# A weighted sum over eight experts: separate two-row tiles replaced by a ten-row ring

## The chip, the cores and the metric

The kernel runs on one core of a Trainium2 chip. The metric is the device time of one execution in microseconds (us). Before the change it is 721.33 us, the median of 9 runs (721.25 to 721.79).

## What is computed

Each of 16 x 1024 = 16384 tokens has eight expert outputs of 512 fp32 values and eight weights. The output is their weighted sum:

```
batch, seq, n_experts, expert_dim = 16, 1024, 8, 512
weights = combine_weights[..., np.newaxis]
return np.sum(expert_outputs * weights, axis=2).astype(np.float32)
```

So 268.4 MB of expert outputs and 0.5 MB of weights are read, and 33.6 MB are written. Every value read is used once, in one multiplication and one addition.

## The kernel before

The tokens are laid over 128 partitions. I call 128 tokens, one on each partition, a **token row**; there are 128 of them, and a row holds 16 KiB of expert outputs per partition. The loop goes over 64 steps of J = 2 rows. A step's input tile `in_t` holds both rows (32 KiB per partition, 4 MiB in all); since a partition's two tokens follow each other in memory, the tile is one contiguous piece of HBM.

*Loads.* `issue_load(m)` (L53 to L63) issues step m's load on SP where m is even and on ACT where it is odd (L56), and a small weight load (8 KB) on POOL (L60). The last two steps' tiles are loaded row by row (L59). Loads are issued three steps ahead (LA = 3) into four buffers, so a load waits until VectorE has finished the step four before it.

*Arithmetic.* For each of the two rows VectorE multiplies expert 0 by its weight (L77, tensor_scalar) and then adds the seven others one by one (L83, scalar_tensor_tensor: out = in * weight + acc). Each of these reads the `acc` that the one before has just written.

*Stores.* The step's result, 4 KiB per partition, is stored by the queue that did not load this step (L92).

*The last two steps* are split between engines: ACT makes the products of experts 4 to 7 in bf16 (L111), VectorE sums experts 0 to 3 (L116, L122), adds the bf16 products in pairs (L130, L135) and to `acc` (L138), and each row is stored by itself from SP (L141).

Each engine works through its own instructions in order. On SP and ACT a load or store that waits holds up what is issued behind it. The code sets no other order.

Of the kernel before, what the change touches and what calls it, by code (L numbers as in the profile page):

```python
# [1 line left out]

# [4 lines left out]


@with_exitstack  # L10
def kernel(
    ctx: ExitStack,
    tc: tile.TileContext,
    expert_outputs: bass.AP,
    combine_weights: bass.AP,
    out: bass.AP,
):
    nc = tc.nc
    fp32 = mybir.dt.float32
    bf16 = mybir.dt.bfloat16  # L20

    B, S, E, D = expert_outputs.shape
    T = B * S
    P = 128
    J = 2
    n_steps = T // (P * J)

    eo_blk = expert_outputs.rearrange("b s e d -> (b s) e d").rearrange(
        "(n p j) e d -> n p j e d", p=P, j=J
    )  # L30
    w_blk = combine_weights.rearrange("b s e -> (b s) e").rearrange(
        "(n p j) e -> n p j e", p=P, j=J
    )
    o_blk = out.rearrange("b s d -> (b s) d").rearrange(
        "(n p j) d -> n p j d", p=P, j=J
    )

    in_pool = ctx.enter_context(tc.tile_pool(name="in_pool", bufs=4))
    w_pool = ctx.enter_context(tc.tile_pool(name="w_pool", bufs=4))
    out_pool = ctx.enter_context(tc.tile_pool(name="out_pool", bufs=4))  # L40
    prod_pool = ctx.enter_context(tc.tile_pool(name="prod_pool", bufs=2))

    ES = E // 2
    K_TAIL = 2

    load_engines = [nc.sync, nc.scalar]

    LA = 3
    in_tiles: list[bass.AP | None] = [None] * n_steps
    w_tiles: list[bass.AP | None] = [None] * n_steps  # L50

    def issue_load(m: int) -> None:
        in_t = in_pool.tile([P, J, E, D], fp32, name="in_t")  # L53
        w_t = w_pool.tile([P, J, E], fp32, name="w_t")
        if m < n_steps - K_TAIL:
            load_engines[m % 2].dma_start(out=in_t, in_=eo_blk[m])  # L56
        else:
            for j in range(J):
                load_engines[m % 2].dma_start(out=in_t[:, j], in_=eo_blk[m, :, j])  # L59
        nc.gpsimd.dma_start(out=w_t, in_=w_blk[m])  # L60
        in_tiles[m] = in_t
        w_tiles[m] = w_t

    for m in range(min(LA, n_steps)):
        issue_load(m)

    for n in range(n_steps):
        if n + LA < n_steps:
            issue_load(n + LA)
        if n >= n_steps - K_TAIL:  # L70
            continue
        in_tile = in_tiles[n]
        w_tile = w_tiles[n]
        acc = out_pool.tile([P, J, D], fp32)

        for j in range(J):
            nc.vector.tensor_scalar_mul(  # L77
                out=acc[:, j, :],
                in0=in_tile[:, j, 0, :],
                scalar1=w_tile[:, j, 0:1],  # L80
            )
            for e in range(1, E):
                nc.vector.scalar_tensor_tensor(  # L83
                    out=acc[:, j, :],
                    in0=in_tile[:, j, e, :],
                    scalar=w_tile[:, j, e : e + 1],
                    in1=acc[:, j, :],
                    op0=mybir.AluOpType.mult,
                    op1=mybir.AluOpType.add,
                )  # L90

        load_engines[(n + 1) % 2].dma_start(out=o_blk[n], in_=acc)  # L92

    tail_steps = list(range(n_steps - K_TAIL, n_steps))
    tail_accs = {}
    tail_prods = {}
    for n in tail_steps:
        acc = out_pool.tile([P, J, D], fp32, name="acc")
        prods = prod_pool.tile([P, J, E - ES, D], bf16, name="prods")
        tail_accs[n] = acc  # L100
        tail_prods[n] = prods

    for j in range(J):
        for n in tail_steps:
            in_tile = in_tiles[n]
            w_tile = w_tiles[n]
            acc = tail_accs[n]
            prods = tail_prods[n]

            for e in range(ES, E):  # L110
                nc.scalar.mul(  # L111
                    out=prods[:, j, e - ES, :],
                    in_=in_tile[:, j, e, :],
                    mul=w_tile[:, j, e : e + 1],
                )
            nc.vector.tensor_scalar_mul(  # L116
                out=acc[:, j, :],
                in0=in_tile[:, j, 0, :],
                scalar1=w_tile[:, j, 0:1],
            )  # L120
            for e in range(1, ES):
                nc.vector.scalar_tensor_tensor(  # L122
                    out=acc[:, j, :],
                    in0=in_tile[:, j, e, :],
                    scalar=w_tile[:, j, e : e + 1],
                    in1=acc[:, j, :],
                    op0=mybir.AluOpType.mult,
                    op1=mybir.AluOpType.add,
                )
            nc.vector.tensor_add(  # L130
                out=prods[:, j, 0:2, :],
                in0=prods[:, j, 0:2, :],
                in1=prods[:, j, 2:4, :],
            )
            nc.vector.tensor_add(  # L135
                out=prods[:, j, 0, :], in0=prods[:, j, 0, :], in1=prods[:, j, 1, :]
            )
            nc.vector.tensor_add(  # L138
                out=acc[:, j, :], in0=acc[:, j, :], in1=prods[:, j, 0, :]
            )  # L140
            nc.sync.dma_start(out=o_blk[n, :, j], in_=acc[:, j, :])  # L141


# [1 line left out]
_INS = ['expert_outputs', 'combine_weights']  # L145
_OUTS = [((16, 1024, 512), 'float32')]


# [23 lines left out]
```

## Time and profile before

| What | Value |
|---|---|
| median of 9 runs | 721.33 us |
| the profiled execution | 721.3 us |
| its span, first to last instruction | 719.5 us |
| VectorE busy | 644.3 us, 1020 instructions |
| ACT busy | 11.4 us |
| L83, one scalar_tensor_tensor of 128x512 f32 | 744 ns, 868 of them |
| L77, one tensor_scalar of 128x512 f32 | 482 ns, 124 of them |
| L111, one ACT multiplication of 128x512 | 710 ns, 16 of them |
| DMA mean over the span | 421 GB/s, 302.63 MB |

The span lies inside the time of the execution; some 1.8 us are around it. "Busy" is the time in which an engine executes, and VectorE, ACT, POOL and SP are separate engines that run beside each other. SP does no arithmetic here, it issues DMAs. All DMAs, whoever issues them, are carried out by the same 16 DMA engines; the profile's DMA share is their mean busy share. A DMA is made of packets; the trace has a record of each packet with its start, length, size and queue, but not with its engine. Where the profile gives what ended an instruction's wait, it names the last event before it.

### The profile page before, as it was taken

The page shows a single profiled execution, that of the slowest core. Times are in us where ns is not written, and L with a number is a line of the kernel's source. Part 1 is how long each engine was busy: PE and PEld are TensorE (multiplying, and loading weights), DVE is VectorE, ACT ScalarE, POOL GpSimd, SP SyncE. Part 2 cuts the span into 40 slices and gives each one's busy share as a digit, 9 for nine tenths or more (in the row PEclk, how much of TensorE's full clock was granted, in tenths as well). Part 3 has the DMA queues.
Part 4 walks back from the last instruction along what each step waited for, and adds up shares of the span by engine and source line. Part 5 has one row for each costly group of instructions (what it writes and reads, how often), then busy time and mean ns, then how long its engine had stood idle before and what let it go on. Part 6 is the DMA issues. An engine that isn't in the chain of part 4 may idle for free.

```text
span 719.5 us, 1532 instructions
## 1 busy us (share of the span) xinstructions
DVE 644.3 (90%) x1020; ACT 11.4 (2%) x17; POOL 35.6 (5%) x68
## 2 busy tenths in 40 slices
DVE  0799999999998999989998999989998999999977
ACT  0000000000000000000000000000000000000023
POOL 1000000000000000000000000000000000000000
DMA  9999999999999999999999999999999999999993
GB/s 380 438 413 443 433 432 431 428 424 427 429 435 445 434 424 427 428 431 428 435 442 431 431 427 427 425 437 441 430 429 429 425 428 434 432 437 433 419 363 139
DMA packets 21068, 302.63 MB, mean 421 GB/s; under 512 B 3136, under 2 KB 4160, under 8 KB 12608
## 3 DMA queue, kind: packets, MB, share of 16 engines
q1 hardware_dynamic: 9792, 151.52, 49.3%
q10 hardware_dynamic: 9216, 150.47, 49.0%
q0 software_dynamic: 2048, 0.53, 0.3%
q14 instruction: 12, 0.10, 0.0%
HBM read 268.96 MB, written 33.55 MB: 420 GB/s over the span
## 4 chain that ended last, share of the span: by engine, by line
DMA 64%; DVE 35%; issue 1%; DVEq 0%; SPq 0%
DMA out_dram<-acc 56%; DVE acc L83 30%; DMA in_t<-in_expert_outputs_dram 8%; DVE acc L77 3%; DVE acc L122 1%; DVE acc L138 0%; DVE prods L130 0%; DVE acc L116 0%; DVE prods L135 0%; DVEq L77 0%; DVEq L116 0%; SPq L92 0%
## 5 line engine op out<-in xcount | busy, mean ns | idle before, releaser
L83 DVE SCALAR_TENSOR_TENSOR acc<-in_t,w_t,acc 128x512 f32<-128x512 f32 x868 | 580.1, 744 | 0.0
L77 DVE TENSOR_SCALAR acc<-in_t,w_t 128x512 f32<-128x512 f32 x124 | 54.6, 482 | 66.2 <-DMA in_t<-in_expert_outputs_dram 43.4
L60 POOL DMA_DIRECT2D w_t<-in_combine_weights_dram x64 | 35.4, 554 | 637.7 <-DVE acc L83 636.9
L111 ACT ACT_TABLE_LOAD x1 | 1.3, 1283 | 690.5 <-DMA in_t<-in_expert_outputs_dram 690.5
L111 ACT ACTIVATE prods<-in_t,w_t 128x512 bf16<-128x512 f32 x16 | 10.1, 710 | 9.3 <-DMA in_t<-in_expert_outputs_dram 9.3
L122 DVE SCALAR_TENSOR_TENSOR acc<-in_t,w_t,acc 128x512 f32<-128x512 f32 x12 | 8.8, 743 | 0.0
L116 DVE TENSOR_SCALAR acc<-in_t,w_t 128x512 f32<-128x512 f32 x4 | 1.9, 480 | 5.3 <-DMA out_dram<-acc 5.3
L138 DVE TENSOR_TENSOR acc<-acc,prods 128x512 f32<-128x512 f32 x4 | 2.7, 685 | 0.0
L130 DVE TENSOR_TENSOR prods<-prods 128x1024 bf16<-128x1024 bf16 x4 | 2.7, 683 | 0.0
L135 DVE TENSOR_TENSOR prods<-prods 128x512 bf16<-128x512 bf16 x4 | 1.7, 416 | 0.0
L156 POOL MEMSET const-float32-0.0<- 128x1 f32 x1 | 0.1, 99 | 0.2 <-issue 0.2
L156 POOL MEMSET const-bfloat16-1.0<- 128x1 bf16 x1 | 0.1, 102 | 0.0
L156 POOL MEMSET const-float32-1.0<- 128x1 f32 x1 | 0.1, 99 | 0.0
L156 POOL MEMSET const-uint8-127<- 128x1 uint8 x1 | 0.1, 99 | 0.0
## 6 DMA issues: line engine op xcount, KB each, us to landing
in_t<-in_expert_outputs_dram ACTq DMA_DIRECT2D x31, 4096.0 KB, 33.5
in_t<-in_expert_outputs_dram SPq DMA_DIRECT2D x31, 4096.0 KB, 33.3
out_dram<-acc ACTq DMA_DIRECT2D x31, 512.0 KB, 33.5
out_dram<-acc SPq DMA_DIRECT2D x31, 512.0 KB, 33.3
in_t<-in_expert_outputs_dram SPq DMA_DIRECT2D x2, 2048.0 KB, 31.2
in_t<-in_expert_outputs_dram ACTq DMA_DIRECT2D x2, 2048.0 KB, 14.0
w_t<-in_combine_weights_dram POOLq DMA_DIRECT2D x64, 8.0 KB, 6.8
out_dram<-acc SPq DMA_DIRECT2D x4, 256.0 KB, 2.7
```

The lines of the kernel that those rows point to most:

```text
L60: nc.gpsimd.dma_start(out=w_t, in_=w_blk[m])
L77: nc.vector.tensor_scalar_mul(out=acc[:, j, :], in0=in_tile[:, j, 0, :], scalar1=w_tile[:, j, 0:1],)
L83: nc.vector.scalar_tensor_tensor(out=acc[:, j, :], in0=in_tile[:, j, e, :], scalar=w_tile[:, j, e : e + 1], in1=acc[:, j, :], op0=mybir.Al ...
L111: nc.scalar.mul(out=prods[:, j, e - ES, :], in_=in_tile[:, j, e, :], mul=w_tile[:, j, e : e + 1],)
L116: nc.vector.tensor_scalar_mul(out=acc[:, j, :], in0=in_tile[:, j, 0, :], scalar1=w_tile[:, j, 0:1],)
L122: nc.vector.scalar_tensor_tensor(out=acc[:, j, :], in0=in_tile[:, j, e, :], scalar=w_tile[:, j, e : e + 1], in1=acc[:, j, :], op0=mybir.Al ...
L130: nc.vector.tensor_add(out=prods[:, j, 0:2, :], in0=prods[:, j, 0:2, :], in1=prods[:, j, 2:4, :],)
L135: nc.vector.tensor_add(out=prods[:, j, 0, :], in0=prods[:, j, 0, :], in1=prods[:, j, 1, :])
L138: nc.vector.tensor_add(out=acc[:, j, :], in0=acc[:, j, :], in1=prods[:, j, 0, :])
L156: nc = _bacc.Bacc("TRN2", target_bir_lowering=False, num_devices=1)
```

## The change

The tiles are replaced by one **ring** of ten token rows in SBUF (`SLOTS = 10`, 160 KiB per partition). Each partition now holds eight consecutive tokens (G = 8) of a group of 1024, so that neighbouring partitions of one load lie 128 KiB apart in HBM.

- *Weights.* All 128 rows' weights are loaded by one DMA at the beginning, on SP, in runs of 256 bytes.
- *Loads.* All on SP, in program order (`pin`): up to four rows (64 KiB per partition) in one DMA, less where the ring or a group of eight ends. Rows 112 to 125 come in pairs, row 126 in two pieces of four experts, row 127 in pieces of 3, 2, 2 and 1 experts. A load waits until VectorE has finished the rows that held its slots.
- *Short rows.* Rows 48 and 72 (`SHORT`) are each loaded as four DMAs of 120, 1, 2 and 5 partitions; their neighbours 49 and 73 are loaded by themselves, with one DMA each.
- *First term.* For rows 0 to 119 ACT multiplies expert 0 by its weight into `acc`, two rows ahead of VectorE.
- *Two chains.* VectorE takes the rows in pairs and alternates between them, term by term.
- *Last eight rows.* For rows 120 to 127 ACT scales an identity matrix by the weights of experts 0 to 2 (three diagonals), TensorE multiplies expert rows by these diagonals in fp32 and sums them in PSUM, and VectorE adds the other five terms, the first of them to the sum in PSUM.
- *Stores.* Eight rows at once (16 KiB per partition) on ACT, then rows 120 to 123 on ACT, 124 and 125 on SP, and 126 and 127 each by itself on SP.

The core of the diff (the old loops, printed above, go altogether; lines that only define names are cut):

```diff
+    G = 8
+    N = T // (P * G)
+    T_P = N * G
+    SLOTS = 10
+    PE_TOKENS = 8
+    SHORT = (48, 72)
+    PE_EXPERTS = 3
...
+    x = expert_outputs.rearrange("b s e d -> (b s) e d").rearrange(
+        "(n p g) e d -> n p g e d", p=P, g=G
     )
...
+    ring = one.tile([P, SLOTS, E, D], fp32, name="ring")
+    acc = one.tile([P, 2 * G, D], fp32, name="acc")
+    w_t = one.tile([P, T_P, E], fp32, name="w_t")
+    ident = one.tile([P, P], fp32, name="ident")
...
+    BULK = 112
+    t = 0
+    while t < BULK:
+        m = min(4, SLOTS - t % SLOTS, G - t % G)
+        if t in SHORT or t - 1 in SHORT:
+            m = 1
+        loads += [(t, m, 0, E)]
+        t += m
+    for t in range(BULK, T_P - 2, 2):
+        loads += [(t, 2, 0, E)]
+    loads += [(T_P - 2, 1, 0, 4), (T_P - 2, 1, 4, 8)]
+    loads += [(T_P - 1, 1, 0, 3), (T_P - 1, 1, 3, 5), (T_P - 1, 1, 5, 7), (T_P - 1, 1, 7, 8)]
...
+    def load_until(t):
+        nonlocal loaded
+        while loaded < len(loads) and loads[loaded][0] + loads[loaded][1] <= t:
+            i, m, e0, e1 = loads[loaded]
...
+            parts = (0, 120, 121, 123, P) if i in SHORT else (0, P)
+            for p0, p1 in zip(parts, parts[1:]):
+                pin(nc.sync.dma_start(out=dst[p0:p1], in_=src[p0:p1]))
+            loaded += 1
...
+    def first(i):
+        s, a = i % SLOTS, i % (2 * G)
+        if i < T_P - PE_TOKENS:
+            pin(nc.scalar.mul(out=acc[:, a], in_=ring[:, s, 0], mul=w_t[:, i, 0:1]))
+            return
+        ps = ps_pool.tile([P, D], fp32, name="ps")
+        for e in range(PE_EXPERTS):
+            diag = diag_pool.tile([P, P], fp32, name="diag")
+            pin(nc.scalar.mul(out=diag, in_=ident, mul=w_t[:, i, e : e + 1]))
+            nc.tensor.matmul(
+                ps, lhsT=diag, rhs=ring[:, s, e], start=e == 0, stop=e == PE_EXPERTS - 1
+            )
+        sums[i] = ps
...
+    def term(i, e):
...
+            before, e0 = (sums[i] if e == PE_EXPERTS else acc[:, a]), PE_EXPERTS
+        if e >= e0:
+            pin(
+                nc.vector.scalar_tensor_tensor(
+                    out=acc[:, a],
+                    in0=ring[:, s, e],
+                    scalar=w_t[:, i, e : e + 1],
+                    in1=before,
+                    op0=mult,
+                    op1=add,
+                )
+            )
...
+    pin(nc.sync.dma_start(out=w_t.rearrange("p (n g) e -> p n (g e)", g=G), in_=w))
+    make_identity(nc, ident)
+    load_until(SLOTS - 2)
+    for i in (0, 1):
+        first(i)
+    for i in range(0, T_P, 2):
+        load_until(i + SLOTS)
+        for k in (i + 2, i + 3):
+            if k < T_P:
+                first(k)
+        for e in range(E):
+            for k in (i, i + 1):
+                term(k, e)
+        end = i + 2
+        if end <= T_P - G and end % G == 0:
+            store(end - G, G, nc.scalar)
+        elif end == T_P - 4:
+            store(end - 4, 4, nc.scalar)
+        elif end == T_P - 2:
+            store(end - 2, 2, nc.sync)
+        elif end == T_P:
+            store(end - 2, 1, nc.sync)
+            store(end - 1, 1, nc.sync)
```

## The prediction, made before the change was run

> **What bounds the kernel now.** I read the page's totals first, then the table of stages, the chain of work that ended last, the timeline of the end, and the trace's records of single DMA packets.
>
> ```profile
> span 719.5 us, 1532 instructions
> ...
> DVE 644.3 (90%) x1020; ACT 11.4 (2%) x17; POOL 35.6 (5%) x68
> ...
> DMA  9999999999999999999999999999999999999993
> ...
> q14 instruction: 12, 0.10, 0.0%
> ```
>
> The line "q14" must be read with its header (packets, MB, share): the code itself is fetched by 12 DMA packets.
>
> ```profile
> core 0: us, DVE busy (x) ACT busy (x) POOL busy (x), PEclk, DMA share, GB/s
> ...
> 360.00:540.00 180.00, 165.14 (x261) 0.00 (x0) 8.55 (x16) 1.00 1.00 430
> ...
> 675.00:692.00 17.00, 16.28 (x27) 1.53 (x2) 0.00 (x0) 1.00 0.91 373
> 692.00:708.60 16.60, 11.27 (x21) 7.33 (x13) 0.00 (x0) 1.00 0.82 322
> 708.60:719.50 10.90, 7.29 (x13) 2.55 (x4) 0.00 (x0) 1.00 0.20 77
> ```
>
> Columns: stretch, its length, busy time of each engine, TensorE clock, DMA share, GB/s. VectorE is 90% busy, but DMA is 100% busy (430 GB/s) until 675 us and only then thins out. The chain gives the pace:
>
> ```profile
> 186.72 0.88 DVE acc L77 x2
> ...
> 629.01 0.88 DVE acc L77 x2
> ```
>
> These are 40 steps of two token rows apart: 442.3/40 = 11.06 us per step, where VectorE needs 2x0.40 + 14x0.663 = 10.08 (in the timeline a chained STT, the scalar_tensor_tensor of L83, starts 0.663 us after the one before, 744 ns long each). So VectorE waits for buffers, and DMA sets the pace.
>
> The packet records say why 11.06. A 2 KiB packet takes 85 ns, 4 KiB 159, 16 KiB 611, 32 KiB 1213: 37.6 ns per KiB plus some 9 ns, of which half overlaps with the neighbour. A 128-partition load leaves eight packets and one completion record on each of 16 engines. Summed, a step is 10.96 us, and fifteen engines keep that pace (their completions come every 10.96). One engine lags: its completion comes 0.8 us after the first at 64 us of the span, 1.8 at 142, 4.2 at 386, 6.5 at 673 (about 5.8 behind the fifteenth). Each step of the lag sits where a 309 ns code packet passes. That lag is the 0.1 us between 10.96 and 11.06.
>
> ```profile
> 690.60 0.82 ACTq L59 DMA_DIRECT2D in_t<-in_expert_outputs_dram  x2
> ...
> 708.59 2.56 ACT L111 ACTIVATE prods<-in_t,w_t 128x512 bf16<-128x512 f32 x4 [2.44 <-DMA in_t<-in_expert_outputs_dram]
> ...
> 715.23 0.69 DVE L138 TENSOR_TENSOR acc<-acc,prods 128x512 f32<-128x512 f32 x1
> ```
>
> The end: ACT issues the last two loads only at 690.6, when an earlier load of that queue has landed; DMA drains meanwhile (33 GB/s from 690.5 to 692.5). The last load lands at 708.6, VectorE ends at 715.9, the last store at 719.5. The profiled execution took 721.3, 1.8 more than its span, and the median is 721.33, so I add 1.8 and need no other correction.
>
> **The change, term by term.** I add up one ordinary DMA engine until the last load has landed, then the tail.
>
> *Start.* The first packet moved at 1.8 us. Now the weights go first on SP: 2048 runs of 256 bytes, 128 per engine. By the fit one costs 9 + 9.4 = 18 ns, together 2.4 us; from above, if the issue of sixteen times as many runs takes sixteen times the 0.33 us of a load, 5.3. I take 2.4, the fit's, since today's 512-byte packets (27 ns) lie on it. The 64 small weight loads on POOL (27 ns per engine each, 1.7 us) go.
>
> *Loads.* The bytes stay: 128 rows x 8 partitions x 16 KiB = 16384 KiB, x 37.6 ns = 616.5 us. One queue instead of two: from 685 to 688 us only SP's ring had loads and ran 16 KiB packets at 611 ns, so one queue loses nothing.
>
> *Stores.* 2048 KiB per engine, 77.1 us; 1920 KiB, 72.2 us, belong to rows up to 119 and lie before the last load, and 2.4 us (rows 120 to 123) too. In packets of 16 KiB instead of 4 KiB there are 152 instead of 512 per engine, which at half of 9 ns saves 1.6. All remaining packets, some 550, cost 2.5 us of such overhead.
>
> *Short rows.* A row as 120+1+2+5 partitions: 128 partitions are 16x8 in the trace; I take 120 as 15x8, so that one engine is spared 8 packets per row, and the eight rest on the first engines, at most 3 on one. Twice: 16x0.611 = 9.8 us spared, at most 6x0.611 = 3.7 us added. If the spared engine is the lagging one, its 5 to 6 us are more than gone, and 3.7 binds instead: 2.1 us better than not splitting. From above: if 120 partitions used fewer engines (eight with 15 packets), 2x7x0.611 = 8.6; if the wrong engine is spared, 3.7+5.8 = 9.5 on the laggard.
>
> Until the last load: 1.8 + 2.4 + 616.5 + 72.2 + 2.4 + 2.5 + 3.7 + 0.6 (last packet to release, as at the first load) = **702.1**. There is no drain as at 690: all loads sit on SP, which issues nothing else until the end, and wait only for ring slots.
>
> *Does the ring keep DMA fed?* A four-row load needs rows ten earlier finished. When four rows land, VectorE needs 0.7 + 28x0.663 = 19.3 us for them; six more rows in the ring are 29 us of loads. So 9.7 us of loads are left at the next issue, less 1.1 us from issue to packets and at most 6 of lag: some 3 us of cover. VectorE has 880 STT, 583 us; per pair of rows 9.3 against 10.9 of DMA. The two chains in turn bring nothing: an STT between foreign instructions in the tail (705.00 to 705.67) also takes 0.67. The multiplications move to ACT: 120x0.71 = 85 us on an idle engine. ACT's stores wait for VectorE with later multiplications behind them, which VectorE needs one pair (9.3 us) later. If the 3 us of cover were gone, each four-row load would add what is missing.
>
> *At nothing.* The identity (POOL) and the 24 scaled copies of it (ACT, at most 24x0.71 = 17 us) are made long before TensorE needs them, ACT's 1.3 us table load falls before the first landing, and the bf16 products and their sums (L111 to L138) go; without that cover a diagonal would delay its product by 0.7.
>
> *Tail.* The first piece of row 127 lands 1.25 MiB before the last, 3.0 us at 432 GB/s: 699.1. Then TensorE makes three products and VectorE, whose order puts row 127's first term second, has nine STT of 0.663 left, 6.1 us with the last one's end. Then 3.6 us, as today from VectorE's end to the span's. No row shows a matmul of 128x512 f32. [...] I take 0.74, the STT's that it replaces: 2.2. Sum: 699.1 + 2.2 + 6.1 + 3.6 = 711.0, + 1.8 = **712.8 us**, against 721.3.
>
> [...] The trace has no matmul and its clock column tells nothing of one. [...] For addresses, loads that were contiguous now step 128 KiB from partition to partition. [...]
>
> **Rivals.**
> 1. *TensorE paces the end (the slow side).* Behind rows 120 and 121 there are six rows (4.85 us each) and 3 MiB of stores (7.3), 36 us, so these rows land at 666. From there 24 products in sequence: 666 + 24m + 0.1 + 6.1 + 3.6 + 1.8. [...] For it: nothing in the trace prices fp32 products; against it: ACT and VectorE do 128x512 in 0.4 to 0.74.
> 2. *Strided loads, or stores beside them, are slower.* Break-even is 8.5/616.5 = 1.4%. For it: from 701.5 to 703.5 us 16 KiB load packets took 864 to 993 ns beside stores. Against it: 16 KiB pieces at 32 KiB pitch at 611. At 3% it gives 731.
> 3. *The split does not do what it says:* the lagging engine is not spared. 5.8 us more: 718.6.
> 4. *Weights at their upper price, products of 1.0 to 1.4 us:* 714 to 718.
> 5. *Less lag, a shorter tail than summed:* 708 to 710.
>
> **Chances.** Forecast (710 to 714.5) 0.45; rival 4 0.14; rival 3 0.10; rival 5 0.12; rival 1 0.08, of which 0.04 is slower and 0.02 the same; rival 2 0.11, of which 0.09 is slower and 0.01 the same; of rival 3 0.01 is the same. A measurement here tells about 0.2%, 1.4 us, from no change. Together: slower 0.13, same 0.04, faster 0.83. The range 708 to 721 leaves out rival 2, rival 1's slow half and the ends.
>
> **What would show it.** DMA share of 1.00 up to about 690 us; last load landing near 702; VectorE's end some 5 us later; a matmul group near 0.7 us; span near 711. A load landing on schedule with VectorE waiting for matmuls speaks for rival 1; load packets over 1213 ns per 32 KiB for rival 2; one engine's completions 5 us late for rival 3. Waits of VectorE with DMA idle in mid-span would refute the ring's cover.

## The result, and the profile after

The changed kernel takes 737.46 us (median of 10 runs, 735.85 to 745.96) against 721.38 us of the kernel before beside it. The ratio is 1.0235 with a 95% interval from 1.0219 to 1.0252: 2.4% slower, where I had forecast 1.2% faster. The profiled execution has a span of 735.1 us, 24.1 us more than the 711.0 that the terms gave.

The page of the changed kernel (busy times, then the 40 slices of 18.4 us each):

```profile
span 735.1 us, 1389 instructions
...
PE 27.7 (4%) x48; PEld 11.2 (2%) x48; DVE 585.7 (80%) x880; ACT 87.0 (12%) x145; POOL 0.7 (0%) x6
...
DMA  9999999999999999999999999999999999999992
GB/s 371 449 414 411 438 449 419 440 421 439 453 420 436 431 259 436 453 423 444 423 419 374 288 423 452 421 421 446 416 457 413 441 428 426 437 429 436 427 386 97
DMA packets 12023, 302.59 MB, mean 412 GB/s; under 512 B 3182, under 2 KB 3182, under 8 KB 4078
```

The row of DMA digits says that nothing is wrong: busy in every slice but the last. The row below says where the time is. The rate falls to 259 in one slice and to 374 and 288 in two others; elsewhere, the start and the end apart, it swings around 430 as before. The first dip is where row 48 is loaded, the second where row 72 is: the two **short rows**. The table of stages around the first dip (stretch, length, busy times, clock, DMA share, GB/s):

```profile
240.00:258.00 18.00, 0.00 (x0) 0.00 (x0) 17.69 (x27) 2.11 (x4) 0.00 (x0) 1.00 0.99 426
258.00:278.00 20.00, 0.00 (x0) 0.00 (x0) 13.96 (x22) 3.28 (x5) 0.00 (x0) 1.00 0.97 269
278.00:300.00 22.00, 0.00 (x0) 0.00 (x0) 14.90 (x23) 0.72 (x1) 0.00 (x0) 1.00 1.00 430
```

A share of 0.97 at 269 GB/s means that the engines are not idle, their packets take longer. The packet records agree: 611 ns is the usual length of a 16 KiB packet; of the 256 of rows 48 and 49 only 82 keep to it, 91 take 1130 to 1280 ns, and the longest takes 1775. Against the usual lengths the excess is 6.8 us per engine from 260 to 280 us and 9.2 from 390 to 420, together 16.0.

The other part that the change rebuilt is the end. The timeline:

```profile
712.10 12.23 PE L104 MATMUL ps<-ring,diag 128*128 128x512 f32 x24 [3.69 <-DMA ring<-in_expert_outputs_dram]
...
716.65 0.75 DVE L117 SCALAR_TENSOR_TENSOR acc<-ring,w_t,ps 128x512 f32<-128x512 f32 x1 [2.15 <-PE ps L104]
...
719.23 0.75 DVE L117 SCALAR_TENSOR_TENSOR acc<-ring,w_t,ps 128x512 f32<-128x512 f32 x1 [1.83 <-PE ps L104]
...
719.89 5.38 DVE L117 SCALAR_TENSOR_TENSOR acc<-ring,w_t,acc 128x512 f32<-128x512 f32 x8
...
725.19 1.40 DVE L117 SCALAR_TENSOR_TENSOR acc<-ring,w_t,ps 128x512 f32<-128x512 f32 x2
...
726.51 5.38 DVE L117 SCALAR_TENSOR_TENSOR acc<-ring,w_t,acc 128x512 f32<-128x512 f32 x8
```

Rows 124 and 125 are there at 711.94; VectorE waits for TensorE's first sum until 716.65 and then has twenty terms, with one more wait of 1.83 us, until 731.9. Each fp32 product is two matmul records, 0.855 us apart in the first part of the burst and 0.43 in the second, where the clock column goes from 0.57 to 1.00 (the third number from the right):

```profile
712.00:716.00 4.00, 3.90 (x5) 1.65 (x6) 2.50 (x4) 1.08 (x4) 0.00 (x0) 0.57 0.70 284
716.00:725.00 9.00, 8.34 (x20) 3.42 (x18) 6.52 (x10) 0.78 (x3) 0.00 (x0) 1.00 0.28 114
```

### The profile page after: what moved, and what is told of

Read it like the earlier page. It is cut to its first block, busy times and chain, and to the rows that moved or that the text cites. A ratio compares the mean times of both kernels' runs of the same rounds, so it can differ in the third digit from the quotient of the medians.

```text
span 735.1 us, 1389 instructions
## 1 busy us (share of the span) xinstructions
PE 27.7 (4%) x48; PEld 11.2 (2%) x48; DVE 585.7 (80%) x880; ACT 87.0 (12%) x145; POOL 0.7 (0%) x6
## 4 chain that ended last, share of the span: by engine, by line
DMA 63%; DVE 32%; ACT 1%; issue 1%; PE 1%; SPq 0%; DVEq 0%; ACTq 0%
DMA ring<-in_expert_outputs_dram 63%; DVE acc L117 32%; ACT acc L98 1%; PE ps L104 1%; ACT L98 0%; DVEq L179 0%; SPq L89 0%; SPq L131 0%; DVEq L117 0%; ACTq L98 0%
## 5 line engine op out<-in xcount | busy, mean ns | idle before, releaser
L117 DVE SCALAR_TENSOR_TENSOR acc<-ring,w_t,acc 128x512 f32<-128x512 f32 x872 | 580.3, 745 | 129.3 <-ACT acc L98 129.3
L98 ACT ACTIVATE acc<-ring,w_t 128x512 f32<-128x512 f32 x120 | 78.0, 711 | 574.4 <-DMA ring<-in_expert_outputs_dram 574.4
L104 PE MATMUL ps<-ring,diag 128*128 128x512 f32 x48 | 27.7, 742 | 696.6 <-DMA ring<-in_expert_outputs_dram 691.4
L104 PEld LDWEIGHTS ps<-ring,diag 128*128 128x128 f32 x48 | 11.2, 239 | 712.4 <-issue 710.7
L117 DVE SCALAR_TENSOR_TENSOR acc<-ring,w_t,ps 128x512 f32<-128x512 f32 x8 | 5.9, 745 | 16.9 <-PE ps L104 16.9
L103 ACT ACTIVATE diag<-ident,w_t 128x128 f32<-128x128 f32 x24 | 7.9, 391 | 29.8 <-DVE acc L117 26.7
```

The costliest lines, as they stand in the source:

```text
L98: pin(nc.scalar.mul(out=acc[:, a], in_=ring[:, s, 0], mul=w_t[:, i, 0:1]))
L103: pin(nc.scalar.mul(out=diag, in_=ident, mul=w_t[:, i, e : e + 1]))
L104: nc.tensor.matmul(ps, lhsT=diag, rhs=ring[:, s, e], start=e == 0, stop=e == PE_EXPERTS - 1)
L117: nc.vector.scalar_tensor_tensor(out=acc[:, a], in0=ring[:, s, e], scalar=w_t[:, i, e : e + 1], in1=before, op0=mult, op1=add,)
```

## The theories

**A.** The four DMAs of a short row are slow because of the partitions that they cover. A row in one DMA of 128 partitions leaves 128 packets and 16 completion records, which I read as eight partitions for each of 16 engines; that a DMA of another shape loses by not having these groups is my guess, no record shows a group. What a run can show is whether the place of the partitions sets the length of the packets. **B.** It is the number of DMAs, or the tiny pieces of 1, 2 and 5 partitions. **C.** Single rows of 16 KiB, 128 KiB apart, are slow, split or not. And for the end, **D:** TensorE's products cost so much at half its clock that VectorE's saving is given back; its rival is that only the late landing of the last rows counts.

## The experiments

Each edit is to the changed kernel unless said otherwise.

### Whole rows

```diff
-            parts = (0, 120, 121, 123, P) if i in SHORT else (0, P)
+            parts = (0, P)
```

> Rows 48 and 72 are still loaded one row at a time, but each by one DMA of 128 partitions instead of four of 120, 1, 2 and 5; all else is the changed kernel. Theory A (the split loads run at half the rate because their 16 engines no longer write 16 separate groups of partitions): no 16 KiB load packet near 1240 ns is left (all near 611), the two dips of the DMA rate are gone, and some 16 us go: 716 to 722 us. Theory B (it is the number of DMAs and the tiny pieces of 1, 2 and 5 partitions): the same 716 to 722. Theory C (single-row loads of 16 KiB at a pitch of 128 KiB are slow, split or not): 735 to 738, unchanged.

Measured: 720.86 us, ratio to before 0.9988 (0.9978 to 0.9998). The split is worth 16.6 us, which the 16.0 of excess packet time account for. Stage and page of this kernel:

```profile
258.00:278.00 20.00, 0.00 (x0) 0.00 (x0) 14.13 (x22) 4.00 (x6) 0.00 (x0) 1.00 0.99 425
```

```profile
DMA packets 12009, 302.59 MB, mean 421 GB/s; under 512 B 3168, under 2 KB 3168, under 8 KB 4064
```

All 16 KiB load packets take 611 to 624 ns, though rows 48, 49, 72 and 73 are still single rows: C falls. The page also shows how the split rows ran: records under 512 bytes are 14 fewer, seven per row. A whole row leaves 16 completion records, so the four pieces left 23, which is 15 + 1 + 2 + 5. That is what I had assumed of the 120 partitions; it was their speed that I had wrong.

### Two halves, and a middle half

```diff
-            parts = (0, 120, 121, 123, P) if i in SHORT else (0, P)
+            parts = (0, 64, P) if i in SHORT else (0, P)
```

> Rows 48 and 72 as two DMAs of 64 partitions (0 to 63, 64 to 127), no tiny piece, no engine spared. Theory A: each half reaches only half of the partition groups, so all 16 KiB packets of these two rows take about 1220 ns; 2 rows x 8 packets x 0.61 = 9.8 us more than with whole rows. Theory B: two DMAs and no tiny piece, at most 2 us more than with whole rows, packets near 611. Theory C: as the changed kernel.

In the second kernel the line is `parts = (0, 32, 96, P) if i in SHORT else (0, P)`.

> Rows 48 and 72 as three DMAs of partitions 0 to 31, 32 to 95 and 96 to 127. [...] Theory B (number of DMAs): three cost more than two, so more than the two halves. If only the count of partitions mattered (64 is slow wherever it lies): all packets about 1220, 9.8 us more.

Measured: the two halves 741.30 us (ratio 1.0271, 1.0235 to 1.0307), the three pieces 733.42 (1.0162, 1.0142 to 1.0182). No piece here is tiny and no engine is spared, yet the halves cost 20.4 us more than whole rows; and three DMAs cost less than two (12.6 us). B falls. A's size for the halves is wrong (20.4 for 9.8). The packet records show one reason: the slow packets hold up the whole loads around them too, packets stay above 1000 ns for some 3 us after the 128 packets of the split row have begun, and in the kernel with three pieces they fall to 692 to 800 ns, which I take for the middle piece, for less than 1 us. For the halves the excess of packet time is 15.7 us over that of whole rows. The 20.4 compares medians, and the halves have only two runs (739.11 and 743.49); the profiled executions, to which the packets belong, are 17.8 us apart (739.11 and 721.34), so some 2 us remain unexplained.

### 120 and 8

```diff
-            parts = (0, 120, 121, 123, P) if i in SHORT else (0, P)
+            parts = (0, 120, P) if i in SHORT else (0, P)
```

> The changed kernel with rows 48 and 72 as two DMAs of 120 and 8 partitions in place of four of 120, 1, 2 and 5. Theory A: the 120 partitions are what costs; 735 to 739 us as the changed kernel, with 16 KiB packets around 1240 ns. Theory B (tiny pieces, number of DMAs): at least half of the 16.6 us between the changed kernel and whole rows is gone, 721 to 729.

Measured: 739.61 us (ratio 1.0251, 1.0233 to 1.0270), as slow as with the tiny pieces. What costs is the piece of 120 partitions, not the tiny ones.

### The same split in the kernel before

```diff
-            load_engines[m % 2].dma_start(out=in_t, in_=eo_blk[m])
+            if m in (24, 36):
+                for p0, p1 in ((0, 120), (120, 121), (121, 123), (123, P)):
+                    load_engines[m % 2].dma_start(out=in_t[p0:p1, 0], in_=eo_blk[m, p0:p1, 0])
+                load_engines[m % 2].dma_start(out=in_t[:, 1], in_=eo_blk[m, :, 1])
+            else:
+                load_engines[m % 2].dma_start(out=in_t, in_=eo_blk[m])
```

> The kernel before, with one row each of steps 24 and 36 loaded as 120, 1, 2 and 5 partitions and the other row of these steps whole. Theory A: the rows' 16 KiB packets at about 1240 ns here too, beside the other queue's load perhaps slowing that as well; 2 x 8 x 0.63 = 10 us or more, so 731 to 738 us. If the loss needs the single queue, the ring or the 128 KiB pitch of the changed kernel: 721 to 724. If the spared engine's lag were what limits the kernel before: 717 to 720.

Measured: 741.84 us, ratio 1.0279 (1.0258 to 1.0299). The loss of 20.3 us needs neither the ring nor the single queue nor the pitch.

### The same number of partitions in two places

This pair has as many DMAs, bytes, engines' packets and partitions in both kernels; only the place differs. It starts from whole rows, and both kernels leave out the other 64 partitions of twelve rows.

```diff
-            parts = (0, P)
+            parts = (0, 64) if i in (36, 60, 84) else (0, P)
```

> From the kernel with whole rows: the loads of rows 36 to 39, 60 to 63 and 84 to 87 bring partitions 0 to 63 only; the other half of these twelve rows is left out. [...] Rival (64 partitions are as fast per packet wherever they lie, the slowness of the split rows comes from several DMAs one after the other): packets stay at 2.42 us and up to 29 us of DMA go, of which VectorE holds up the most; 700 to 715.

In the second kernel it is `(32, 96)`.

> The same with partitions 32 to 95 in place of 0 to 63, as many partitions and bytes; the rest of the twelve rows is left out. [...] If the number of partitions decides, the same as partitions 0 to 63 in packets and in time.

Measured: partitions 0 to 63, 735.15 us (ratio 1.0187, 1.0164 to 1.0210); partitions 32 to 95, 694.03 us (0.9617, 0.9598 to 0.9637). The stage in which rows 36 to 39 are loaded, first with 0 to 63, then with 32 to 95:

```profile
195.00:215.00 20.00, 0.00 (x0) 0.00 (x0) 14.53 (x22) 2.56 (x4) 0.00 (x0) 1.00 0.90 207
```

```profile
195.00:215.00 20.00, 0.00 (x0) 0.00 (x0) 17.57 (x27) 5.12 (x8) 0.00 (x0) 1.00 1.00 426
```

207 against 426 GB/s. The 64 KiB packets take 5.00 to 5.29 us in the first kernel (195 to 205 us, median 5.10) and 2.42 in the second. With half of these rows' data on partitions 0 to 63 the kernel takes longer than with all of it (735.15 against 720.86 us). This decides for A as far as the place goes. The place in SBUF also sets the place in HBM, since partition p of these loads reads 128 KiB behind partition p - 1: the two kernels read rows 4 MiB apart, and no run separates the two. That the split rows cost as much in the kernel before, where the neighbours lie 32 KiB apart, speaks against HBM. That 120 partitions are slow for the same reason is an inference, since no record names an engine or a place: many of their packets take twice as long too (1130 to 1280 for 611).

### TensorE at the end

```diff
-    PE_TOKENS = 8
+    PE_TOKENS = 0
```

> From the kernel with whole rows: TensorE has no part, the last eight rows are done as all others (ACT the first term, VectorE seven). Theory D (an fp32 product of 128x512 costs 1.71 us at the half clock and 0.86 at the full, so the sums come so late that they give back what VectorE saves): the end comes within 2 us of the kernel with whole rows, 719 to 723 us. Rival (the three terms are saved, as the forecast had it): the last four rows cost VectorE two more terms each, 8 x 0.663 = 5.3 us, 726.

```diff
+    def pe_experts(i):
+        return 5 if i < T_P - 4 else PE_EXPERTS
...
-        for e in range(PE_EXPERTS):
+        for e in range(pe_experts(i)):
...
-                ps, lhsT=diag, rhs=ring[:, s, e], start=e == 0, stop=e == PE_EXPERTS - 1
+                ps, lhsT=diag, rhs=ring[:, s, e], start=e == 0, stop=e == pe_experts(i) - 1
...
-            before, e0 = (sums[i] if e == PE_EXPERTS else acc[:, a]), PE_EXPERTS
+            before, e0 = (sums[i] if e == pe_experts(i) else acc[:, a]), pe_experts(i)
```

> From the kernel with whole rows: for rows 120 to 123 TensorE sums five experts instead of three, for 124 to 127 three as before. [...] If the late end lies only in the loads of the last rows (a lagging DMA engine), 720 to 722, unchanged; if TensorE is late with the longer sums, more than that.

The pool of diagonals also grows, from 12 buffers to 16.

Measured, both with whole rows: without TensorE 719.15 us (ratio 0.9965, 0.9952 to 0.9978), which is 1.7 us less than with it; with five experts for rows 120 to 123, 717.48 us (0.9950, 0.9933 to 0.9966), 3.4 less. More work for TensorE made the end earlier. Part of both differences is not TensorE's: in the profiled executions rows 124 and 125 land 1.1 us (without TensorE) and 1.4 us (five experts) earlier than with whole rows, and loads were that much ahead before TensorE's first product. From this landing to the end of the span it is 23.7 us with whole rows, 22.5 without TensorE and 21.3 with five experts, so 1.2 and 2.4 us are the end's own. The burst for rows 124 to 127, whole rows first, then with five experts:

```profile
695.85 12.92 PE L104 MATMUL ps<-ring,diag 128*128 128x512 f32 x24 [4.91 <-DVE acc L117]
```

```profile
682.75 10.52 PE L107 MATMUL ps<-ring,diag 128*128 128x512 f32 x20 [2.02 <-issue]
694.44 10.54 PE L107 MATMUL ps<-ring,diag 128*128 128x512 f32 x24 [1.17 <-DMA ring<-in_expert_outputs_dram]
```

After a gap of 4.9 us the 24 records take 12.92 us, after one of 1.2 us 10.54: 0.44 us each, from the start. D holds; the earlier landing has the rest. Other gaps: after the 2.0 us before the 20 records at 682.75 the clock is 0.50 from 684.1 to 687.5 us, and after 2.8 and 2.9 us in the next two kernels it falls to half as well, while gaps of 1.7 us in the first of them and 1.4 in the second left it full. Here 2.0 us without work were enough. The two kernels' intervals overlap, so that five experts are better than no TensorE is likely, not shown.

### Row by row

```diff
+        if i < T_P - PE_TOKENS:
+            order = [(k, e) for e in range(E) for k in (i, i + 1)]
+        else:
+            order = [(k, e) for k in (i, i + 1) for e in range(E)]
-        for e in range(E):
-            for k in (i, i + 1):
-                term(k, e)
+        for k, e in order:
+            term(k, e)
```

> From the kernel with whole rows and five experts on TensorE for rows 120 to 123: VectorE takes the last eight rows one after the other instead of two in turn. Theory D: VectorE no longer stands 1.8 us idle behind the first term of row 125, which TensorE finishes 2.6 us after row 124's; the end comes 1.5 to 2 us earlier: 715 to 716.5 us. If the last load's landing sets the end, not VectorE's queue, it stays at 717 to 718. Theory A says nothing on this.

Measured: 719.40 us (ratio 0.9959, 0.9946 to 0.9973), not earlier. The wait in front of row 125 is gone, but the chain itself is slower. VectorE at the end, row by row, then two rows in turn (the kernel with five experts):

```profile
699.71 0.75 DVE L120 SCALAR_TENSOR_TENSOR acc<-ring,w_t,ps 128x512 f32<-128x512 f32 x1 [5.02 <-PE ps L107]
700.50 3.11 DVE L120 SCALAR_TENSOR_TENSOR acc<-ring,w_t,acc 128x512 f32<-128x512 f32 x4
703.53 0.74 DVE L120 SCALAR_TENSOR_TENSOR acc<-ring,w_t,ps 128x512 f32<-128x512 f32 x1
```

```profile
700.53 5.38 DVE L120 SCALAR_TENSOR_TENSOR acc<-ring,w_t,acc 128x512 f32<-128x512 f32 x8
705.83 1.40 DVE L120 SCALAR_TENSOR_TENSOR acc<-ring,w_t,ps 128x512 f32<-128x512 f32 x2
```

Four terms in 3.11 us are 0.79 from start to start; eight in 5.38 are 0.66. From the landing of rows 124 and 125 to the end of the span it is 23.1 us, against 21.3 with two rows in turn. In this run TensorE's burst also began cold (12.23 us after a gap of 2.8), so the time alone would decide nothing.

### A version that beats both

The edit is to the kernel with five experts; the pool of diagonals has 10 buffers here, and a new pool of six holds the bf16 products.

```diff
-        return 5 if i < T_P - 4 else PE_EXPERTS
+        return 5
...
+            if i >= T_P - 4 and e >= 2:
+                prod = prod_pool.tile([P, D], bf16, name="prod")
+                pin(nc.scalar.mul(out=prod, in_=ring[:, s, e], mul=w_t[:, i, e : e + 1]))
+                lhsT, rhs = ident16, prod
+            else:
+                diag = diag_pool.tile([P, P], fp32, name="diag")
+                pin(nc.scalar.mul(out=diag, in_=ident, mul=w_t[:, i, e : e + 1]))
+                lhsT, rhs = diag, ring[:, s, e]
+            nc.tensor.matmul(ps, lhsT=lhsT, rhs=rhs, start=e == 0, stop=e == pe_experts(i) - 1)
```

> From the kernel with whole rows and five experts on TensorE for rows 120 to 123: rows 124 to 127 also leave only three terms to VectorE; TensorE sums experts 0 and 1 through diagonals as before, and experts 2 to 4 as bf16 products that ACT makes, through a bf16 identity. Theory D: at the full clock a row costs TensorE 2 x 0.86 + 3 x some 0.22 = 2.4 us instead of 2.6 and VectorE 2.0 instead of 3.3, so VectorE has no queue of terms left when the last piece lands near 705 us, and the end comes up to 4 us earlier: 713 to 715.5. If the last landing or TensorE is the later one already, 716.5 to 718.5.

Measured: 715.39 us, ratio 0.9916 (0.9902 to 0.9929), 0.8% faster than the kernel before and the fastest here that computes everything. VectorE ends 2.3 us earlier than with five experts, at 710.3, though the last load lands 0.3 us later:

```profile
702.98 0.81 PE L116 MATMUL ps<-prod,ident 128*128 128x512 bf16 x3
...
706.86 0.75 DVE L127 SCALAR_TENSOR_TENSOR acc<-ring,w_t,ps 128x512 f32<-128x512 f32 x1 [1.34 <-PE ps L116]
707.53 2.73 DVE L127 SCALAR_TENSOR_TENSOR acc<-ring,w_t,acc 128x512 f32<-128x512 f32 x4
```

It waits 1.34 us for row 127's sum now, that is, for its first five experts to land (at 705.0) and be summed, and has no queue of terms left.

## Why the prediction was wrong

The difference of 24.1 us between the forecast's span and the measured one goes to these steps. The last load's last completion is at 724.2 us in the changed kernel and at 707.9 with whole rows; the forecast had 702.1.

- **"Short rows": the step that failed, 16.3 us** (724.2 - 707.9). I counted packets and took 611 ns for each, and bounded the split by how many packets an engine might get. I asked which engine moves them, and not where they are written. The runs show that many take 1130 to 1280 ns instead, that they slow the whole loads beside them, and, for 64 partitions, that the place decides.
- *The relief reached the engine that I had in mind.* In the changed kernel one engine completes row loads 8.5 us ahead of twelve others after the second split row (431.9 against 440.4 us); with whole rows one engine lags there (440.8 against 438.4). Its lead over the median engine then shrinks from 7.4 us at 452 us to 2.8 at 707, as a lagging engine's must. So the spared engine is the lagging one, and rival 3 falls. But three engines are late instead, I take it those with extra pieces, and at the last load one is 6.3 us behind the fifteenth where I had 3.7: almost the lag that the split was to remove.
- *The lag and the fifteen engines, 5.8 us.* With whole rows fifteen engines are done at 700.6, 2.2 us later than my terms give without the 3.7; 1.2 us of it are slow packets in the first 10 us, the rest I did not break down. The laggard comes 7.3 us after them, where the forecast, which took the laggard for relieved, had 3.7 for the engine with the extra pieces.
- **"Tail", 2.0 us.** From the last completion to the end it is 10.9 us, forecast 8.9. The mis-sized term is the product: 0.74 taken (VectorE's time for a term; no run shows it for TensorE), 0.86 at the full clock and 1.71 at half measured, with the second price ahead of rows 124 to 127. I priced only row 127; that rows 124 and 125 leave a queue of twenty terms was not in the sum.
- *Right:* the weights (2.6 us for 2.4). The single queue and the pitch of 128 KiB cost nothing: 64 KiB packets take 2.42 us, 37.8 ns per KiB, as the 32 KiB packets before (1213 ns). Stores of 16 KiB beside loads take 611 ns, so rival 2 falls. The ring kept DMA fed (share 1.00 from 540 to 690 us).
- *Right for a reason that I had not seen:* alternating two chains changes nothing against the kernel before, because that one alternates already. Its timeline has L77 twice and then L83 fourteen times, at 0.663. A chain by itself takes 0.79.
- *Not right:* ACT's table load stood behind the first landing (25.54 us), 1.3 us in which VectorE waited. DMA, which sets the pace, was not held up by it (share 0.99 from 20 to 70 us).
- *Two readings of the old trace that were off, without weight in the sum:* DMA moves 33 GB/s from 690.5 to 691.5 us only, 147 over the 2 us that I named, and the 16 KiB load packets from 701.5 to 703.5 us take 621 to 1641 ns, not 864 to 993.

My slow rivals were TensorE, which was late but cheap, and slow strided loads. The right kind of failure, load packets that take longer, stood there with the wrong cause.

## What to carry to other kernels

In these runs a DMA's price was not only its bytes and its packets per engine but the partitions that it wrote: before a load is cut below 128 partitions, measure one such piece and read the length of its packets, since here the busy share was 0.97 at 269 GB/s and 0.90 at 207. A repair for one lagging engine must cost the other fifteen less than the lag, here 7 us; this one cost 16. TensorE work in short bursts has to be priced at the half clock where pauses come before it, here pauses of 2.0 us and more, and filling the pause can be cheaper than doing less (717.48 against 719.15 us, with intervals that overlap).

## What the runs showed of the hardware that I had not expected

- Loads on partitions 0 to 63 move 207 GB/s, on 32 to 95 426, with the same number of partitions; 64 KiB packets take 5.10 and 2.42 us.
- A slow load also slows whole loads around it: beside row 72 a single 64 KiB packet took up to 5.4 us in the changed kernel, where with whole rows none took over 3.1 after the first 10 us.
- One of 16 DMA engines lags by 5.8 to 7.3 us over 700 us also where POOL issues no DMA; the steps of the lag in the kernel before sit at the code packets of some 309 ns.
- The TensorE clock fell to half after pauses of 2.0 us and more: in the changed kernel for 6.8 us (698.8 to 705.7, within and after a pause of 5.2) and for 3.4 us (712.5 to 715.9, after one of 3.7), with five experts for 3.4 us after one of 2.0; after 1.2, 1.4 and 1.7 us it stayed full (pauses as the profile has them, with modelled ends of the matmuls).
- An fp32 product of 128x512 is two matmul records, together 0.86 us at the full and 1.71 at the half clock; bf16 ones stand 0.22 us apart at the full clock (three in 0.81 us, the last 0.38 long).
